# The second weight pair as seven half-size products, with GpSimd rebuilding two operand blocks

## The chip, the cores and the metric

The kernel runs on one core of a Trainium2 chip. Its time is device microseconds of one execution; the runs shown before are three, and their median is used. Five engines work side by side, each through a queue of its own in program order: TensorE (PE in the profile, its weight loads PEld), VectorE (DVE), ScalarE (ACT), GpSimd (POOL) and SyncE (SP), which here issues nearly all DMAs.

## The reference

One layer (DEPTH is 1, so only the short-convolution mixer runs), on 1024 tokens of 1024 channels, in float32:

```python
def short_conv_mixer(u, w_in, conv_w, w_out):
    z, bg, cg, v = jnp.split(u @ w_in.astype(u.dtype), 4, axis=-1)
    y = bg * causal_dwconv(cg * v, conv_w) * jax.nn.silu(z)
    return y @ w_out.astype(u.dtype)

h = x
u = rms_norm(h, pre_norm[i])
m = short_conv_mixer(u, sc_w_in[j], sc_conv_w[j], sc_w_out[j])
h = h + rms_norm(m, post_norm[i])
```

`w_in` is 1024 x 8192: four types (z, bg, cg, v) of 2048 columns. `conv_w` has 3 taps, `w_out` is 2048 x 1024.

## The kernel before

**Precision.** TensorE multiplies in a rounded 32-bit form (F32R). Each operand is held as two parts, a high part (a rounded copy, made by ScalarE) and a low part (what is left, a subtraction on VectorE); each product is three matmuls: high x high, high x low, low x high. One matmul is 128x128 weights against 128x512.

**Pairs and seven products.** The 2048 channels are 16 chunks of 128. For each chunk there are two weight pairs: p even holds types cg and v, p odd holds z and bg; so 32 pairs, `PAIRS`. Of a pair, the two types (rows n = 0, 1) times the two halves of the 1024 input channels make a 2x2 block of weights, and the two halves of the channels times the two halves of the tokens make a 2x2 block of the normalised input. The product of the two is done as in Strassen's and Winograd's scheme, with seven products `a, b, c, e, d, f, g` (ORDER) in place of eight: `product(p, i)` issues 4 x 3 matmuls. The weights enter as the plain row 0 (part 0, for a and b), as sums that GpSimd makes (`add_s`, L123 to L137; part 1 for c and e, part 2 for d and f) and as half of row 1 (part 3, for g); `split_w` (L143 to L155) splits each into its parts with one cast on ScalarE (L140) and one subtraction on VectorE (L141). The input side has seven operands too, in `UH[i]` and `UL[i]`: a and b are the two channel halves for the first 512 tokens, f and e come from the last 512, c, d and g are sums of these blocks. `snap`, `after` and `first_chunk` combine the products' banks and go on to the gate, the convolution and the next stage.

**The head.** The first two pairs, p = 0 and 1, are not done by seven products but plainly, in 2 types x 2 halves of the tokens x 8 slices x 3 = 96 matmuls each (`plain`, `high_plain`, `low_plain`), since the input's sums aren't there yet. The first four tiles of 128 tokens are loaded, normalised and transposed first (`turn`); a and b follow from them; the plain products of pair 0 on the first half of the tokens run on TensorE. Meanwhile the last four tiles get their squares (`square` on ScalarE at L323, `square_v` on VectorE at L326), the root and the reciprocal (`pre_rstd`, L86 to L105, with three tiny VectorE operations L103, L104, L105), and are scaled by these (L457 on VectorE, L459 on ScalarE). Then four rounds follow: `turn2(kk)` transposes two slices of the four tiles (8 small matmuls at L344), and `second(kk)` (L473 to L478) makes slices of the operands e and f from them. `rebuild(q)` (L405) adds the high and the low part of a or b into `bt`, which lies in the memory of the first input tiles `xa`; `second` subtracts `bt`'s first half from the fresh slice, `t_sub` makes c, d and g's sources of both halves. `t_split` splits these in two parts.

**Order.** The tile framework runs with `manual_schedule`: on every engine the instructions stand in program order, and only waits for data and for buffers are put in. Buffers come from pools with a fixed number of slots: tag "raw" has three (a pair's weights, 1 MB each), tag "sum" one (the weights' sums), tag "w8" three and "w4" two (split weights); a new tile waits until the slot's last reader is done. TensorE's program order in the head is: plain products of pair 0 on the first token half; four times (12 matmuls of pair 1, `turn2`, `second`); the rest of pair 1; pair 0 on the second token half; then pair 2 by seven products, and so on through pair 31, and the output product, which is done in the same seven-product form.

Of the kernel before, what the change touches and what calls it, by code (L numbers as in the profile page):

```python
# [8 lines left out]
F32 = mybir.dt.float32  # L9
F32R = mybir.dt.float32r  # L10
# [8 lines left out]
def kernel(  # L19
# [16 lines left out]
    nc = tc.nc  # L36
# [76 lines left out]
    def fetch(p, rows=(0, 1)):  # L113
        if p >= len(PAIRS):
            return
        c, tys = PAIRS[p]
        if p not in raws:
            raws[p] = raw.tile([P, 2, NK, P], F32, tag="raw", name=f"raw_{p}")
        for n in rows:
            c0 = tys[n] * CI + c * P  # L120
            nc.sync.dma_start(raws[p][:, n], wiv[:, :, c0 : c0 + P])
# [21 lines left out]
    def split_w(p, part):  # L143

        if p >= len(PAIRS):
            return
        n = 2 * HB if part < 3 else HB
        tag = "w8" if part < 3 else "w4"
        t = wp.tile([P, 2, n], F32R, tag=tag, name=f"w{part}_{p}", bufs=3 if part < 3 else 2)
# [172 lines left out]
    def square(t):  # L322
        nc.scalar.activation(junk, xs[t], AF.Square, scale=D ** -0.5, accum_out=sq[:, t : t + 1])  # L323
# [39 lines left out]

    plain_w = {}

    def tile_plain(p, n):
        if (p, n) == (1, 1):
            plain_w[p, n] = raw.tile([P, 2, D], F32R, tag="sum", name=f"wn{n}_{p}", bufs=1)
        else:
            plain_w[p, n] = wp.tile([P, 2, D], F32R, tag="w8", name=f"wn{n}_{p}", bufs=3)  # L370

    def high_plain(p, n):
        tile_plain(p, n)
        nc.scalar.copy(plain_w[p, n][:, 0], flat(raws[p][:, n]))

    def low_plain(p, n):
        t = plain_w[p, n]
        nc.vector.tensor_sub(t[:, 1], flat(raws[p][:, n]), t[:, 0].bitcast(F32))

    def plain(p, n, half, part, kks=range(4)):  # L380
# [4 lines left out]
        for kk in kks:  # L385
            k = part * KH + kk
            hi, lo = (w[:, h, k * P : (k + 1) * P] for h in (0, 1))
            nc.tensor.matmul(ps, hi, UH[i][:, kk], start=part == 0 and kk == 0, stop=False, skip_group_check=True)  # L388
            nc.tensor.matmul(ps, hi, UL[i][:, kk], start=False, stop=False, skip_group_check=True)  # L389
            nc.tensor.matmul(ps, lo, UH[i][:, kk], start=False, stop=kk == KH - 1, skip_group_check=True)  # L390
# [9 lines left out]
    def rebuild(q, js=(0, 1)):  # L400

        for j in js:
            ks = slice(2 * j, 2 * j + 2)
            i = "ab"[q]
            nc.vector.tensor_add(bt[:, q, ks], UH[i][:, ks].bitcast(F32), UL[i][:, ks].bitcast(F32))  # L405


    stir(WARM)
# [22 lines left out]
    high_plain(0, 1)  # L431
    low_plain(0, 1)
    for k in range(KH):
        plain(0, 0, 0, 0, [k])
        for t in (2, 3) if k < KH - 1 else range(TH):
            turn(k + KH, t)
    read_k(4)
# [16 lines left out]
    for j in range(TH):  # L454
        x2 = xs[TH + j]
        if j % 2:
            nc.vector.tensor_scalar(x2, x2, rs2[:, j : j + 1], None, op0=ALU.mult)  # L457
        else:
            nc.scalar.activation(x2, x2, AF.Copy, scale=rs2[:, j : j + 1])  # L459
    low_plain(1, 1)  # L460
    rebuild(0, [1])


    def turn2(kk):
        for k in (kk, kk + KH):
            for t in range(TH, NT):
                turn(k, t)
# [9 lines left out]
        low("f", kk, p22, kk + KH)  # L477
        nc.vector.tensor_sub(by_tile(UL["e"][:, kk]), t1, by_tile(UH["e"][:, kk]).bitcast(F32))  # L478
# [12 lines left out]
    def halves(a, j):  # L491
        return a[:, 2 * j : 2 * j + 2].rearrange("p k (t l) -> p k t l", t=TH)

    def t_split(i, src):
        for j in range(2):
            hi, lo = (halves(u[i], j) for u in (UH, UL))
            nc.scalar.copy(hi, src(j))
            nc.vector.tensor_sub(lo, src(j), hi.bitcast(F32))

    def t_sub(q):  # L500
        for j in range(2):
# [22 lines left out]
    pc = bank("pcw")  # L524
    nc.tensor.transpose(pc[:, : TAPS * NC], cw_rows, ident[: TAPS * NC, : TAPS * NC])
    nc.scalar.copy(cw, pc[:, : TAPS * NC])
# [25 lines left out]

    def first_chunk(i):

        if i == "b":
            g = gpad[:, TAPS - 1 : TAPS - 1 + HB]
            nc.scalar.copy(g, banks[0, 0, 0])
            nc.vector.tensor_mul(g, banks[0, 1, 0], g)
            nc.vector.tensor_mul(gpad[:, TAPS - 1 + HB :], sn[0, 0], sn[0, 1])
        elif i == "c":  # L560
            conv(0)
        elif i == "d":
            cv, z = cvs.pop(0), banks[1, 0, 0]
            nc.scalar.activation(z, z, AF.Silu)
            nc.scalar.activation(sn[1, 0], sn[1, 0], AF.Silu)
            nc.vector.tensor_mul(cv[:, :HB], banks[1, 1, 0], cv[:, :HB])
            nc.vector.tensor_mul(cv[:, :HB], z, cv[:, :HB])
            nc.gpsimd.tensor_mul(cv[:, HB:], cv[:, HB:], sn[1, 1])
            nc.gpsimd.tensor_mul(cv[:, HB:], cv[:, HB:], sn[1, 0])
            y_done(0, cv)  # L570


# [34 lines left out]
    END = len(PAIRS) - 1  # L607
    TODO = {p: p // 2 - 2 for p in range(4, 4 + 2 * CH - 2, 2)}
    TODO[2 * CH + 1] = CH - 1
    for p in range(2, len(PAIRS)):  # L610
        q, prev = p + 1, p // 2 - 1
        for i in ORDER:
# [180 lines left out]
```

## Time and profile before

| | |
|---|---|
| three runs | 795.88, 795.68, 795.34 us; median 795.68 |
| profiled execution | 796.12 us, span of its instructions 794.3 us |
| matmuls and other TensorE instructions | 3514, busy 99% of the span |
| VectorE, ScalarE, GpSimd busy | 67%, 39%, 34% |
| mean granted TensorE clock | 0.998 |
| DMA | 114.38 MB, 144 GB/s on average |

A row of the timeline is: start (us from the span's start), duration, engine, line, operation, what is written <- what is read, shape, count, and in brackets how long the engine stood idle before it and what ended that. Rows of one kind in a row are merged (x2 and more). A row's duration includes the time in which the instruction itself is held up inside the engine; a next one of the same engine can start a little before the end of the one before. Matmuls show 0.39 us each but follow each other more closely, as they are pipelined. In the table of stretches the columns are the stretch, its length, then for each engine the busy time and count, the granted clock, the DMA share and GB/s.

### The profile page before, as it was taken

Reading aid. Unit: us, or ns where it says so; the run is one execution under the profiler, and the core shown is the slowest. Engines: PE = TensorE matmul, PEld = TensorE weight load, DVE = VectorE, ACT = ScalarE, POOL = GpSimd, SP = SyncE. Lnnn points to the kernel's source line nnn. Section 1 sums busy time; section 2 is a strip of 40 time slices with the busy share of each in tenths; the row PEclk is TensorE's granted clock in tenths of the full one; section 3 lists DMA queues with packets and bytes.
Section 4 is the critical chain, followed back from the end, with each engine's and each line's share of the span. In section 5 each row is a group of like instructions: output and inputs, shape, how many; then the busy total and the mean of one; then the engine's idle time right before and its main releaser. Section 6 shows DMA issues by size and latency. Waiting matters only on the chain.

```text
span 794.3 us, 9053 instructions
## 1 busy us (share of the span) xinstructions
PE 785.7 (99%) x3514; PEld 652.1 (82%) x3514; DVE 534.8 (67%) x580; ACT 306.6 (39%) x421; POOL 271.2 (34%) x182
## 2 busy tenths in 40 slices
PE   9999999999999999999999999999999999999996
PEld 8888888888888888888888888888888888888885
DVE  5899676767676767676757666666666857633766
ACT  6636333342433333333333332323333536544441
POOL 0034534443444444447444444444344000000020
PEclk9999999999999999999999999999999999999999
DMA  9600361517070707165433334142515659555237
GB/s 317 161 0 1 93 198 54 199 53 229 23 242 10 252 26 226 45 207 174 130 94 106 109 91 145 54 142 57 161 39 178 233 193 419 204 203 212 106 111 260
DMA packets 94282, 114.38 MB, mean 144 GB/s; under 512 B 2920, under 2 KB 68512, under 8 KB 92192
## 3 DMA queue, kind: packets, MB, share of 16 engines
q1 hardware_dynamic: 94224, 113.81, 44.1%
q8 instruction: 27, 0.44, 0.2%
q14 instruction: 15, 0.12, 0.0%
q10 hardware_dynamic: 16, 0.00, 0.0%
HBM read 84.44 MB, written 29.36 MB: 143 GB/s over the span
## 4 chain that ended last, share of the span: by engine, by line
PE 94%; DMA 3%; DVE 1%; ACT 1%; SPq 0%; POOLq 0%; POOL 0%; issue 0%; DVEq 0%; ACTq 0%
PE px L186 14%; PE px L187 14%; PE px L188 14%; PE pv L186 7%; PE pv L187 7%; PE pv L188 7%; PE py L186 3%; PE py L187 3%; PE py L188 3%; PE po_x L673 3%; PE po_x L672 3%; PE po_x L671 3%; PE pp L389 2%; PE pp L390 2%; PE pp L388 2%; DMA xr<-in_x 2%
## 5 line engine op out<-in xcount | busy, mean ns | idle before, releaser
L141 DVE TENSOR_TENSOR w<-sum,w 128x1024 fp32r<-128x1024 f32 x60 | 89.8, 1498 | 75.1 <-ACT w L140 75.1
L141 DVE TENSOR_TENSOR w<-raw,w 128x1024 fp32r<-128x1024 f32 (+1 forms) x60 | 96.6, 1609 | 5.2 <-ACT w L140 5.2
L140 ACT CAST w<-sum 128x1024 fp32r<-128x1024 f32 x60 | 62.9, 1048 | 56.6 <-issue 54.5
L548 DVE SCALAR_TENSOR_TENSOR cv<-gpad,cw,cv 128x1024 f32<-128x1024 f32 x32 | 63.2, 1976 | 19.7 <-ACT cv L546 19.1
L140 ACT CAST w<-raw 128x1024 fp32r<-128x1024 f32 (+1 forms) x60 | 49.9, 832 | 62.6 <-PE py L188 62.6
L133 POOL TENSOR_TENSOR sum<-raw 128x512 f32<-128x512 f32 x30 | 39.1, 1302 | 90.5 <-PE pp L390 51.5
L225 POOL TENSOR_TENSOR gpad<-snc,sne 128x512 f32<-128x512 f32 x15 | 19.4, 1295 | 139.6 <-DVE snc L220 139.6
L136 POOL TENSOR_TENSOR sum<-raw 128x512 f32<-128x512 f32 x30 | 59.8, 1992 | 0.0
L220 DVE TENSOR_TENSOR snc<-pv,snc 128x512 f32<-128x512 f32 x30 | 20.7, 691 | 54.1 <-PE pv L188 54.1
L217 POOL TENSOR_TENSOR sne<-sne,cv 128x512 f32<-128x512 f32 x15 | 19.4, 1293 | 103.1 <-DVE sne L215 103.1
L137 POOL TENSOR_TENSOR sum<-raw,sum 128x512 f32<-128x512 f32 x30 | 53.9, 1796 | 0.0
L711 POOL TENSOR_TENSOR acc<-acc,xr 128x512 f32<-128x512 f32 x4 | 6.9, 1722 | 133.0 <-DVE acc L710 133.0
L186 PE MATMUL px<-u_g,w 128*128 128x512 f32 x120 | 46.8, 390 | 0.0
L188 PE MATMUL px<-u_g,w 128*128 128x512 f32 x120 | 46.7, 390 | 0.0
L188 PE MATMUL pv<-u_f,w 128*128 128x512 f32 x120 | 46.7, 390 | 0.0
L186 PE MATMUL pv<-u_f,w 128*128 128x512 f32 x120 | 46.7, 389 | 0.0
L187 PE MATMUL pv<-u_f,w 128*128 128x512 f32 x120 | 46.7, 389 | 0.0
L187 PE MATMUL px<-u_g,w 128*128 128x512 f32 x120 | 46.7, 389 | 0.0
L187 PE MATMUL py<-u_b,w 128*128 128x512 f32 x120 | 46.7, 389 | 0.0
L186 PE MATMUL py<-u_b,w 128*128 128x512 f32 x120 | 46.7, 389 | 0.0
L187 PE MATMUL px<-u_a,w 128*128 128x512 f32 x120 | 46.7, 389 | 0.0
L186 PE MATMUL px<-u_a,w 128*128 128x512 f32 x120 | 46.7, 389 | 0.0
(248 smaller groups left out, 2092.5 us busy)
## 6 DMA issues: line engine op xcount, KB each, us to landing
raw<-in_sc_w_in SPq DMA_DIRECT2D x64, 512.0 KB, 5.9
y_d<-cv SPq DMA_DIRECT2D x16, 512.0 KB, 3.3
t<-in_sc_w_out SPq DMA_DIRECT2D x8, 1024.0 KB, 5.8
t_d<-t SPq DMA_DIRECT2D x8, 1024.0 KB, 4.5
s_d<-s SPq DMA_DIRECT2D x8, 768.0 KB, 3.5
s<-y_d SPq DMA_DIRECT2D x8, 512.0 KB, 5.0
xr<-in_x SPq DMA_DIRECT2D x8, 512.0 KB, 4.6
out<-acc SPq DMA_DIRECT2D x12, 256.0 KB, 2.4
```

The costliest lines, as they stand in the source:

```text
L133: nc.gpsimd.tensor_add(s[:, 1], a21, a22)
L136: nc.gpsimd.tensor_sub(s[:, 2], a11, a21)
L137: nc.gpsimd.tensor_sub(s[:, 3], a12, s[:, 0])
L140: nc.scalar.copy(hi, src)
L141: nc.vector.tensor_sub(lo, src, hi.bitcast(F32))
L186: nc.tensor.matmul(ps, lo, UH[i][:, k], start=first and k == 0, stop=False, skip_group_check=True)
L187: nc.tensor.matmul(ps, hi, UL[i][:, k], start=False, stop=False, skip_group_check=True)
L188: nc.tensor.matmul(ps, hi, UH[i][:, k], start=False, stop=last, skip_group_check=True)
L548: nc.vector.scalar_tensor_tensor(cv, gpad[:, j : j + L], tap(c, j), cv, op0=ALU.mult, op1=ALU.add)
L671: nc.tensor.matmul(ps, lo, u[:, 0, k], start=first, stop=False, skip_group_check=True)
L672: nc.tensor.matmul(ps, hi, u[:, 1, k], start=False, stop=False, skip_group_check=True)
L673: nc.tensor.matmul(ps, hi, u[:, 0, k], start=False, stop=last, skip_group_check=True)
```

## The change

Pair 0 stays plain. Pair 1 is done by seven products, in an order interleaved with the second half of pair 0: product a, `turn2(0)`, product b, `turn2(1)`, then pair 0's products on the second token half in four pieces (`plain_late(kk)`, one slice of f and of e each, with `turn2(2)` and `turn2(3)` between them), then c, e, d, f, g. The weights of pair 1 therefore go through `add_s` and `split_w`, where `high_plain` and `low_plain` stood; parts 1 and 2 of them are put into slots of tag "raw". `rebuild` is on GpSimd in place of VectorE, all four steps of it, three of them earlier in the order (`rebuild(0, [1])` now stands ahead of the scaling, and `rebuild(1)`, which stood behind the operand d, just behind the scaling). The sums of pair 2 (`add_s(2, ...)`) move up between the rounds. The load of pair 2's weights stands later in program order, and the small transpose that prepares the convolution's taps stands ahead of product a. `t_halves` is the two steps of `t_split`, so that the sum of product e's and d's banks can be put between them for g. `first_chunk` follows the new names, and the remaining splits of pair 2 move into it.

```diff
+        if p == 1 and part in (1, 2):
+            t = raw.tile([P, 2, n], F32R, tag="raw", name=f"w{part}_{p}")
+        else:
+            t = wp.tile([P, 2, n], F32R, tag=tag, name=f"w{part}_{p}", bufs=3 if part < 3 else 2)
...
     fetch(1)
     nc.sync.dma_start(cw_rows, conv_w[0].rearrange("t (c p) -> (t c) p", p=P))
-    fetch(2)
...
     def rebuild(q, js=(0, 1)):
...
-            nc.vector.tensor_add(bt[:, q, ks], UH[i][:, ks].bitcast(F32), UL[i][:, ks].bitcast(F32))
+            nc.gpsimd.tensor_add(bt[:, q, ks], UH[i][:, ks].bitcast(F32), UL[i][:, ks].bitcast(F32))
...
     plain(0, 0, 0, 1)
     plain(0, 1, 0, 1)
-    high_plain(1, 0)
     rebuild(0, [0])
+    add_s(1, 0)
     square(TH)
     square_v(TH + 1)
-    low_plain(1, 0)
+    split_w(1, 0)
     square(TH + 2)
     square_v(TH + 3)
     rs2 = pre_rstd(list(range(TH, NT)))
-    high_plain(1, 1)
+    add_s(1, 1)
+    rebuild(0, [1])
     for j in range(TH):
...
-    low_plain(1, 1)
-    rebuild(0, [1])
+    rebuild(1)
+    split_w(1, 1)
+    pc = bank("pcw")
+    nc.tensor.transpose(pc[:, : TAPS * NC], cw_rows, ident[: TAPS * NC, : TAPS * NC])
+    nc.scalar.copy(cw, pc[:, : TAPS * NC])
...
-    for kk, (n, part) in enumerate(((0, 0), (1, 0), (0, 1), (1, 1))):
-        plain(1, n, 0, part)
-        turn2(kk)
-        second(kk)
-        if part == 0:
-            plain_snap(1, n)
+    def plain_late(kk):
+
+        for part in (1, 0):
+            for n in (0, 1):
+                plain(0, n, 1, part, [kk], first=part == 1 and kk == 0, last=part == 0 and kk == KH - 1)
+
+    product(1, "a")
+    snap(1, "a")
+    turn2(0)
+    second(0)
+    split_w(1, 3)
+    fetch(2)
+    product(1, "b")
+    after(1, "b")
+    turn2(1)
+    second(1)
+    split_w(1, 2)
+    plain_late(0)
+    turn2(2)
+    second(2)
+    add_s(2, 0)
+    add_s(2, 1)
+    plain_late(1)
+    turn2(3)
+    second(3)
+    plain_late(2)
+    plain_late(3)
...
-    for kks in ((0, 1, 2), (3,)):
-        for n in (0, 1):
-            plain(1, n, 1, 0, kks)
-    for n in (0, 1):
-        plain(1, n, 1, 1)
     t_split("c", lambda j: cols4(1, j))
     t_sub(0)
     t_split("d", lambda j: halves(bt[:, 0], j))
-    plain_add(1, 0)
-    rebuild(1)
-    plain_add(1, 1)
+    product(1, "c")
+    snap(1, "c")
     t_sub(1)
     new_u("g")
-    add_s(2, 0)
+    product(1, "e")
+    snap(1, "e")
+    product(1, "d")
+    g_hi, g_lo = t_halves("g", lambda j: halves(bt[:, 1], j))
+    g_hi(0)
+    g_lo(0)
+    g_hi(1)
+    nc.vector.tensor_add(sn[1, "e"], banks[1, "x"], sn[1, "e"])
+    g_lo(1)
+    product(1, "f")
+    product(1, "g")
     split_w(2, 0)
-    t_split("g", lambda j: halves(bt[:, 1], j))
...
+    plain_add(0, 0)
+    plain_add(0, 1)
+    nc.vector.tensor_add(sn[1, "c"], banks[1, "v"], sn[1, "c"])
     head.close()
...
     fetch(3)
-
-    for n in (0, 1):
-        for part in (0, 1):
-            plain(0, n, 1, part)
-    add_s(2, 1)
-    split_w(2, 3)
-    split_w(2, 1)
-    split_w(2, 2)
-    plain_add(0, 0)
-    plain_add(0, 1)
```

More of the change, by code (lines that the diff above doesn't have):

```diff
@@ L364 @@
     plain_w = {}
[L366 to L370, printed above, removed]
     def high_plain(p, n):
-        tile_plain(p, n)
+        plain_w[p, n] = wp.tile([P, 2, D], F32R, tag="w8", name=f"wn{n}_{p}", bufs=3)
         nc.scalar.copy(plain_w[p, n][:, 0], flat(raws[p][:, n]))
@@ L378, in low_plain, with plain @@
         nc.vector.tensor_sub(t[:, 1], flat(raws[p][:, n]), t[:, 0].bitcast(F32))
-    def plain(p, n, half, part, kks=range(4)):
+    def plain(p, n, half, part, kks=range(4), first=None, last=None):
         i = "abef"[2 * half + part]
@@ L384, in plain @@
         ps, w = banks[p, n, half], plain_w[p, n]
-        for kk in kks:
+        first = part == 0 if first is None else first
+        last = part == 1 if last is None else last
+        for j, kk in enumerate(kks):
             k = part * KH + kk
             hi, lo = (w[:, h, k * P : (k + 1) * P] for h in (0, 1))
-            nc.tensor.matmul(ps, hi, UH[i][:, kk], start=part == 0 and kk == 0, stop=False, skip_group_check=True)
+            end = last and j == len(kks) - 1
+            nc.tensor.matmul(ps, hi, UH[i][:, kk], start=first and j == 0, stop=False, skip_group_check=True)
             nc.tensor.matmul(ps, hi, UL[i][:, kk], start=False, stop=False, skip_group_check=True)
-            nc.tensor.matmul(ps, lo, UH[i][:, kk], start=False, stop=kk == KH - 1, skip_group_check=True)
+            nc.tensor.matmul(ps, lo, UH[i][:, kk], start=False, stop=end, skip_group_check=True)
     def plain_snap(p, n):
@@ L433 @@
     for k in range(KH):
-        plain(0, 0, 0, 0, [k])
+        plain(0, 0, 0, 0, [k], first=k == 0)
         for t in (2, 3) if k < KH - 1 else range(TH):
@@ L492, in halves, with t_halves @@
         return a[:, 2 * j : 2 * j + 2].rearrange("p k (t l) -> p k t l", t=TH)
+    def t_halves(i, src):
+        hi, lo = ((lambda j, u=u: halves(u[i], j)) for u in (UH, UL))
+        return (
+            lambda j: nc.scalar.copy(hi(j), src(j)),
+            lambda j: nc.vector.tensor_sub(lo(j), src(j), hi(j).bitcast(F32)),
+        )
     def t_split(i, src):
+        hi, lo = t_halves(i, src)
         for j in range(2):
-            hi, lo = (halves(u[i], j) for u in (UH, UL))
-            nc.scalar.copy(hi, src(j))
-            nc.vector.tensor_sub(lo, src(j), hi.bitcast(F32))
+            hi(j)
+            lo(j)
     def t_sub(q):
@@ L553, in first_chunk @@
     def first_chunk(i):
-        if i == "b":
+        if i == "":
             g = gpad[:, TAPS - 1 : TAPS - 1 + HB]
@@ L609 @@
     TODO[2 * CH + 1] = CH - 1
+    first_chunk("")
     for p in range(2, len(PAIRS)):
```

27 lines of the change are left out of this document (14 added, 13 removed).

## The prediction

> **What bounds the kernel now.** I read the page first, then the table of stretches, the waits of TensorE (PE), and the timelines of the first 64 us engine by engine.
>
> ```profile
> PE 785.7 (99%) x3514; PEld 652.1 (82%) x3514; DVE 534.8 (67%) x580; ACT 306.6 (39%) x421; POOL 271.2 (34%) x182
> ```
>
> ```profile
> PE pp L389 <- DVE u_a L357: 0.5, 1, 0.5
> ```
>
> ```profile
> 63.89 0.39 PE L186 MATMUL px<-u_a,w 128*128 128x512 f32 x1
> ...
> 66.61 0.39 PE L186 MATMUL py<-u_b,w 128*128 128x512 f32 x1
> ```
>
> TensorE is busy for 99% of the span. The second line is the only wait of TensorE in 13:700 us. So the kernel is a dense line of matmuls: one removed saves its slot, and a hole in the line costs its full length. The slot is the distance of the third fence: twelve matmuls from 63.89 to 66.61, so 0.227 us each (the 0.39 us of one overlaps its neighbours).
>
> **What is removed.** The pair takes 2 types x 2 halves of the tokens x 8 slices x 3 = 96 matmuls now and 7 products x 4 slices x 3 = 84 afterwards. 12 x 0.227 = **-2.72 us**. The transposes and the rest of TensorE's list keep their number. That is all the change can gain while TensorE stays fed.
>
> **What is moved to GpSimd (POOL).** The four rebuild steps of 128x1024 leave VectorE (DVE), and four sums of 128x512 for this pair are new, as the weights now enter as sums. GpSimd waits for nothing there but its data, so it runs as soon as it can. In what order VectorE and GpSimd get on beside each other is decided by these rows:
>
> ```profile
> 67.61 1.30 POOL L133 TENSOR_TENSOR sum<-raw 128x512 f32<-128x512 f32 x1 [6.51 <-DVE w L141]
> ```
>
> ```profile
> 52.84 1.56 POOL L133 TENSOR_TENSOR sum<-raw 128x512 f32<-128x512 f32 x1 [51.51 <-PE pp L390]
> 54.48 2.15 POOL L134 TENSOR_TENSOR sum<-sum,raw 128x512 f32<-128x512 f32 x1
> 56.60 2.27 POOL L136 TENSOR_TENSOR sum<-raw 128x512 f32<-128x512 f32 x1
> ```
>
> ```profile
> 53.16 2.32 DVE L405 TENSOR_TENSOR xa<-u_b 128x1024 f32<-128x1024 f32 x1
> 55.41 0.68 DVE L398 TENSOR_TENSOR sp<-pp,sp 128x512 f32<-128x512 f32 x1
> ```
>
> A sum alone takes 1.30 us. A VectorE operation of 128x1024 with both inputs in SBUF alone takes 1.2 (21.59, below), and its successor starts 1.14 later. Side by side they take turns, whole instructions at a time: the VectorE one of 53.16 needs 2.32 = what is left of GpSimd's (to 54.4) + 1.1; GpSimd's of 54.48 needs 2.15 = what is left of VectorE's (to 55.4) + 1.25. The one of 55.41 reads one input from PSUM and keeps its 0.68 beside a busy GpSimd. Even a tiny operation queues, as the end of the kernel shows:
>
> ```profile
> 772.70 1.73 POOL L711 TENSOR_TENSOR acc<-acc,xr 128x512 f32<-128x512 f32 x1 [2.02 <-DVE acc L710]
> ```
>
> ```profile
> 773.51 0.15 DVE L99 TENSOR_SCALAR hr_post<-r_post 128x1 f32<-128x1 f32 x1
> 773.58 0.87 DVE L101 SCALAR_TENSOR_TENSOR nt_post<-r_post,ve_post 128x1 f32<-128x1 f32 x1
> 774.48 0.16 DVE L105 SCALAR_TENSOR_TENSOR rs_post<-nt_post,hr_post 128x1 f32<-128x1 f32 x1
> ```
>
> L101, one element per partition, ends at 774.45, just as GpSimd's operation does at 774.43; L105, of the same kind but behind it, takes 0.16. L99, with one tensor input, doesn't wait (0.15). So where GpSimd has a queue, every VectorE operation with two SBUF inputs, however small, waits for one GpSimd operation: 1.27 us for 512 elements, and about 2.5 for a rebuild of 1024. The 2.5 is an estimate, twice the 512 row; bounds are 1.8 (a fixed share of it paid once) and 3.0.
>
> **Who waits behind that.** The second half of the tokens is normalised at just this place. Before:
>
> ```profile
> 21.59 1.21 DVE L405 TENSOR_TENSOR xa<-u_a 128x1024 f32<-128x1024 f32 x1
> 22.72 1.22 DVE L326 SCALAR_TENSOR_TENSOR u_e<-xb 128x1024 fp32r<-128x1024 f32 x1
> ...
> 23.86 1.22 DVE L378 TENSOR_TENSOR wn<-raw,wn 128x1024 fp32r<-128x1024 f32 x1
> 25.00 1.22 DVE L326 SCALAR_TENSOR_TENSOR u_e<-xb 128x1024 fp32r<-128x1024 f32 x1
> ...
> 26.94 0.15 DVE L103 TENSOR_TENSOR nt_pre<-r_pre 128x4 f32<-128x4 f32 x1
> 27.13 0.16 DVE L104 TENSOR_TENSOR nt_pre<-nt_pre,ve_pre 128x4 f32<-128x4 f32 x1
> 27.33 0.17 DVE L105 SCALAR_TENSOR_TENSOR rs_pre<-nt_pre,hr_pre 128x4 f32<-128x4 f32 x1
> 27.53 1.42 DVE L457 TENSOR_SCALAR xb<-xb,rs_pre 128x1024 f32<-128x1024 f32 x2
> ```
>
> ```profile
> 23.45 1.06 ACT L323 ACTIVATE junk<-xb 128x1024 f32<-128x1024 f32 x1
> 24.41 0.19 ACT L323 ACTIVATION_READ_ACCUMULATOR junk<-xb 128x1 f32 x1
> ...
> 27.53 2.19 ACT L459 ACTIVATE xb<-xb,rs_pre 128x1024 f32<-128x1024 f32 x2
> ```
>
> ```profile
> 29.99 1.03 PE L344 MATMUL pk<-ident,xb 128*128 128x128 f32 x8
> ```
>
> The chain is: squares, root, reciprocal, three tiny VectorE operations (L103 to L105, each with two SBUF inputs), then the scaling, half on ScalarE (ACT, to 29.72), then the transposes at 29.99. TensorE's cover is one block of 12 matmuls, which ends at 29.99 and in the new order (product a, behind one small transpose) at about 30.1. It hides 0.3 us of delay and no more.
>
> GpSimd's new list starts once the transposes that read the tile it overwrites are done:
>
> ```profile
> 18.20 1.05 PE L342 MATMUL pk<-rows,xa 128*128 128x128 f32 x8
> ```
>
> ```profile
> 10.64 3.84 SPq L121 DMA_DIRECT2D raw<-in_sc_w_in  x2
> ```
>
> ```profile
> DMA to landing us min/median/max: 5.7/9.2/10.7
> ```
>
> So from 19.3. The pair's weights, issued from 10.64 with at most 10.7 us to landing, are there at about 21.8 (issue of the second at 11.1). With turns taken as above, estimated from the rows:
>
> - GpSimd: first rebuild 19.3-21.8. VectorE: first square 21.8-23.0. GpSimd: sum 1 23.0-24.2, sum 2 24.3-25.6, as VectorE has nothing ready: its weight rounding waits for ScalarE's cast, which is now behind a square (ends about 24.6).
> - VectorE: weight rounding 25.6-26.7. GpSimd: sum 3 to 28.0. VectorE: second square to 29.1. GpSimd: sum 4 to 30.4.
> - The root and the reciprocal need no turn (29.1-29.8). L103 at 30.4. Rebuild 2 to 33.0. L104. Rebuild 3 to 35.7. L105, ready at 35.9. Rebuild 4 to 38.4.
> - ScalarE scales two tiles, 35.9 to 38.1 (2.19 before). The transposes start at **38.1** instead of 30.1, a hole of **+8.0 us** in TensorE's line.
>
> **Is the hole closed later?** No: TensorE has no slack from there to 760. Nor does it grow, by VectorE's load from the scaling to the first use of c:
>
> ```profile
> 31.13 0.74 DVE L473 SCALAR_TENSOR_TENSOR xb<-pk,gcol,xa 128x512 f32<-128x512 f32 x1
> ...
> 33.31 0.68 DVE L478 TENSOR_TENSOR u_e<-xb,u_e 128x512 fp32r<-128x512 f32 x1
> ```
>
> Four rounds of 2.9 (31.13 to 33.99), three roundings at 1.14 (the sums' two parts, c's first half), and two operations of 512 elements at 0.6: about 16.2 us, against four groups of transposes of 0.9 (the 1.03 of 29.99 overlaps its successor) and 60 matmuls of 0.227 = 17.2 on TensorE. That is covered by 1.1 us, and more while TensorE runs at half clock (next). The sums for the third pair wait for the one sum buffer and so come after this pair's rounding. The loads of the fourth and fifth weight pair now wait for buffers that this pair's products e and f read, but are wanted one pair and more later. Both cost nothing as long as TensorE is the late one; without that cover, each GpSimd operation in VectorE's way costs 1.27.
>
> **The clock.** These rows say what a hole does to TensorE's clock:
>
> ```profile
> 1.05 5.48 PE L320 MATMUL pw<-idle 128*128 128x128 f32 x28 [1.05 <-DVE idle L280]
> 6.87 1.83 PE L342 MATMUL pk<-rows,xa 128*128 128x128 f32 x14 [0.34 <-DVE rows L412]
> ```
>
> ```profile
> 785.00:794.30 9.30, 2.65 (x12) 1.87 (x10) 4.74 (x15) 0.98 (x3) 0.00 (x0) 0.80 0.61 212
> ```
>
> In the last 9.3 us TensorE works 2.65 and the mean clock is 0.80. If idle means half, that is 3.7 us at half, so the clock falls about 3 us after the last matmul. A hole of 8 us is longer. At the start 28 matmuls take 5.48 us and 14 later ones 1.83 (0.11 apart): with 0.21 for a slow one, 20 were slow, so the slow stretch lasts 4.4 us. At half speed that loses **+2.2 us**. The Trainium skill ("TensorE: Matmul & The Clock Gate", What's actually happening) has the clock restored after one busy window of about 3.4 us; by that this term would be an estimated 1.7 and the forecast 0.5 lower. The trace's 4.4 is used.
>
> **Sum**: -2.72 + 8.0 + 2.2 = **+7.5 us**. The profiled execution is 796.12 (span 794.3), 0.44 above the median of the runs, 795.68; so I expect 803.6 for a profiled one and **803.2** as the time.
>
> **Rivals.**
>
> 1. *VectorE's scaling (L457) waits as well.* It has one tensor input, as L99, which didn't wait; but its two of 1024 take 1.42, twice the pace of the others, so it may use both paths. Then the scaling behind rebuild 4 ends at 39.8 instead of 38.1: 804.9. The Trainium skill ("SBUF — State Buffer", Who interferes with whom) says this of tensor_scalar in its two-port modes, and that the later one fully blocks; no run here shows L457 beside GpSimd. Chance 0.20.
> 2. *The tiny operations slip between GpSimd's.* For it: they hold the path for 0.15 only. Against: 773.58. Then the root's result comes at 30.4, the transposes start at 32.6, hole 2.5, no cold clock: 795.5. But the three rebuilds left then fall on the VectorE rounds, where up to one wait of 2.5 stays uncovered: 798.0. Chance 0.13.
> 3. *Faster.* The squares find gaps and the root's result is there by 27.9, when ScalarE's 2.19 still ends under product a. That is the point from which it decides. For it: VectorE is rid of the 1.14 of rebuild that stood ahead of the first square (21.59). Against: GpSimd has over 10 us of queue by then. Gain 2.72: 793.0. Chance 0.13.
> 4. *VectorE stays behind.* Slow rebuilds (3.0) and the sums for pair three hit c, d and g too: two or three waits of 1.27 more, 806 to 807. Chance 0.04.
>
> **Numbers.** Forecast 0.50. About 0.2% (1.6 us) is what a measurement can tell from no change, so "same" is 794.1 to 797.3: a third of rival 2, 0.05 with its edges. Faster is rival 3, 0.13; slower 0.82. The range runs from 796.5 (between the ends of rival 2) to 806.5: rebuilds of 1.8 us give -1.0, of 3.0 +1.4, a clock that never drops -2.2, rival 1 +1.7. What it leaves out is rival 3 and bits of rivals 2 and 4.
>
> **What would show it.** In the new profile TensorE should have one wait of 8 us ahead of L344, its clock under 1.0 in the slice behind it, L103 to L105 at up to 2.5 us each with GpSimd busy between 19 and 38, and matmul groups 12 fewer. The prediction is wrong if the transposes start by 31, if the root's operations keep their 0.15 beside GpSimd, or if holes appear at c or g instead.

## The result and the profile after

| | before | after |
|---|---|---|
| median of five runs | 795.68 us (795.34 to 796.19) | 804.46 us (804.07 to 806.75) |
| profiled execution, span | 796.12, 794.3 | 804.46, 802.7 |
| mean granted clock | 0.998 | 0.994 |

The changed kernel is slower, 1.0116 times the time before (95% interval 1.0101 to 1.0131), 8.8 us by the medians and 8.3 us by the two profiled executions. Each ratio further down is against the kernel before on the same chip, where its median was 795.77, 796.07 or 796.10 us. In the changed file the lines have moved by some places: the transposes of the second half of the tokens are L346 (L344 before), the products' matmuls L189 to L191 (L186 to L188), the scaling L458 and L460 (L457 and L459).

The page of after, busy time and the granted clock in 40 slices:

```profile
PE 785.1 (98%) x3502; PEld 649.8 (81%) x3502; DVE 538.4 (67%) x579; ACT 308.6 (38%) x424; POOL 286.2 (36%) x190
...
PEclk9899999999999999999999999999999999999999
```

TensorE has the 12 matmuls less (3514 to 3502) and is busy for the same time, but in a longer span. Its waits in 13:700 us (us in total, times, longest):

```profile
PE pk L346 <- ACT xb L460: 8.2, 2, 7.9
PE pv L189 <- ACT sne L197: 0.5, 1, 0.5
```

Before, there was one wait of 0.5, at the first operands; it is still there and not shown. New is one hole of 7.9 us ahead of the transposes, named after ScalarE's scaling. ScalarE itself waited (all engines' waits, after):

```profile
ACT xb L460 <- DVE rs_pre L105: 7.7, 1, 7.7
ACT sne L197 <- POOL cv L593: 3.8, 1, 3.8
```

So the reader goes on to VectorE, the timeline of after:

```profile
29.01 1.06 DVE L97 TENSOR_SCALAR ve_pre<-sq 128x4 f32<-128x4 f32 x1
...
30.18 2.19 DVE L99 TENSOR_SCALAR hr_pre<-r_pre 128x4 f32<-128x4 f32 x1
32.28 0.15 DVE L103 TENSOR_TENSOR nt_pre<-r_pre 128x4 f32<-128x4 f32 x1
32.47 2.19 DVE L104 TENSOR_TENSOR nt_pre<-nt_pre,ve_pre 128x4 f32<-128x4 f32 x1
34.69 2.26 DVE L105 SCALAR_TENSOR_TENSOR rs_pre<-nt_pre,hr_pre 128x4 f32<-128x4 f32 x1
36.98 1.42 DVE L458 TENSOR_SCALAR xb<-xb,rs_pre 128x1024 f32<-128x1024 f32 x2
```

and of GpSimd beside it:

```profile
27.77 2.27 POOL L137 TENSOR_TENSOR sum<-raw,sum 128x512 f32<-128x512 f32 x1
30.00 2.34 POOL L405 TENSOR_TENSOR xa<-u_a 128x1024 f32<-128x1024 f32 x1
32.30 4.63 POOL L405 TENSOR_TENSOR xa<-u_b 128x1024 f32<-128x1024 f32 x2
```

The ends stand next to each other. VectorE's L97 ends at 30.07, as GpSimd's last sum does at 30.04; L99, on four elements per partition, ends at 32.37 and the rebuild of 30.00 at 32.34. L104 ends at 34.66 and L105 at 36.95; GpSimd's last two rebuilds fill 32.30 to 36.93. L99, L104 and L105 each take the time of one rebuild, about 2.2 us in place of 0.16. The scaling then runs with GpSimd out of the way, in its usual 1.42.

TensorE's timeline of after from the transposes on, and the start of the fourth pair before:

```profile
38.19 0.69 PE L346 MATMUL pk<-ident,xb 128*128 128x128 f32 x2 [7.87 <-ACT xb L460]
39.23 1.54 PE L346 MATMUL pk<-ident,xb 128*128 128x128 f32 x6 [0.35 <-ACT xb L460]
...
44.00 1.03 PE L346 MATMUL pk<-ident,xb 128*128 128x128 f32 x8
...
47.62 1.03 PE L346 MATMUL pk<-ident,xb 128*128 128x128 f32 x8
...
51.23 1.03 PE L346 MATMUL pk<-ident,xb 128*128 128x128 f32 x8
...
57.81 0.39 PE L189 MATMUL px<-u_c,w 128*128 128x512 f32 x1
...
71.42 0.39 PE L189 MATMUL px<-u_a,w 128*128 128x512 f32 x1
...
91.44 0.39 PE L189 MATMUL px<-u_a,w 128*128 128x512 f32 x1
```

```profile
82.93 0.39 PE L186 MATMUL px<-u_a,w 128*128 128x512 f32 x1
```

From these rows the 8.34 us between the spans can be laid out. Pair 2's product a starts 7.53 later than before (71.42 against 63.89). That is the hole of 7.87, less 2.72 for the 12 matmuls, plus 2.42: from the first transposes to product c there are 19.62 us (38.19 to 57.81), where TensorE's own list is 17.2 (the prediction's count of transposes and matmuls; a run below shows 17.23). These three make 7.57. Pair 2 then takes 20.02 where it took 19.04 (63.89 to 82.93): +0.98. From there to the end 0.17 is regained.

The 2.42 lies almost wholly in the first of the four rounds: 38.19 to 44.00 is 5.81, and the two behind it are 3.62 and 3.61, which is the eight transposes and twelve matmuls at their usual pace. The clock at this place (stretch, length, PE, PEld, DVE, ACT, POOL busy, clock, DMA), after:

```profile
35.00:40.00 5.00, 1.46 (x6) 1.06 (x7) 3.37 (x3) 3.02 (x3) 1.93 (x1) 0.52 0.00 0
40.00:45.00 5.00, 5.00 (x25) 4.28 (x24) 4.34 (x6) 2.52 (x6) 0.00 (x0) 0.80 0.01 2
```

0.80 over 40 to 45 is 2.0 us at half, so the clock is low until about 42.0, 3.8 us into the work. So far all of it reads like the prediction. Whether the low clock is what costs the 2.42 is asked below.

### The profile page after: what moved, and what is told of

It reads as the page before. It is cut to its first block, busy times and chain, and to the rows that moved or that the text cites. A ratio compares the mean times of both kernels' runs of the same rounds, so it can differ in the third digit from the quotient of the medians.

```text
span 802.7 us, 9045 instructions
## 1 busy us (share of the span) xinstructions
PE 785.1 (98%) x3502; PEld 649.8 (81%) x3502; DVE 538.4 (67%) x579; ACT 308.6 (38%) x424; POOL 286.2 (36%) x190
## 4 chain that ended last, share of the span: by engine, by line
PE 92%; DVE 2%; issue 2%; DMA 2%; ACT 1%; POOL 1%; SPq 0%; DVEq 0%; POOLq 0%
PE px L189 13%; PE px L190 13%; PE px L191 13%; PE pv L189 7%; PE pv L190 7%; PE pv L191 7%; PE po_x L704 4%; PE po_x L703 4%; PE po_x L702 4%; PE py L189 3%; PE py L190 3%; PE py L191 3%; PE po_v L704 2%; PE po_v L703 2%; PE po_v L702 2%
## 5 line engine op out<-in xcount | busy, mean ns | idle before, releaser
L141 DVE TENSOR_TENSOR w<-sum,w 128x1024 fp32r<-128x1024 f32 x62 | 91.7, 1478 | 82.1 <-ACT w L140 82.0
L141 DVE TENSOR_TENSOR w<-raw,w 128x1024 fp32r<-128x1024 f32 (+1 forms) x62 | 99.1, 1600 | 7.0 <-ACT w L140 7.0
L140 ACT CAST w<-sum 128x1024 fp32r<-128x1024 f32 x62 | 65.0, 1048 | 58.3 <-issue 54.5
L133 POOL TENSOR_TENSOR sum<-raw 128x512 f32<-128x512 f32 x31 | 40.1, 1294 | 71.9 <-DVE w L141 69.8
L136 POOL TENSOR_TENSOR sum<-raw 128x512 f32<-128x512 f32 x31 | 62.6, 2020 | 0.0
L189 PE MATMUL pv<-u_f,w 128*128 128x512 f32 x124 | 48.4, 390 | 0.5 <-ACT sne L197 0.5
L189 PE MATMUL py<-u_b,w 128*128 128x512 f32 x124 | 48.7, 393 | 0.0
L191 PE MATMUL py<-u_b,w 128*128 128x512 f32 x124 | 48.5, 391 | 0.0
L190 PE MATMUL py<-u_b,w 128*128 128x512 f32 x124 | 48.5, 391 | 0.0
L189 PE MATMUL px<-u_a,w 128*128 128x512 f32 x124 | 48.4, 390 | 0.0
L189 PE MATMUL px<-u_g,w 128*128 128x512 f32 x124 | 48.3, 390 | 0.0
L190 PE MATMUL px<-u_g,w 128*128 128x512 f32 x124 | 48.3, 389 | 0.0
L191 PE MATMUL px<-u_g,w 128*128 128x512 f32 x124 | 48.3, 389 | 0.0
L190 PE MATMUL pv<-u_f,w 128*128 128x512 f32 x124 | 48.2, 389 | 0.0
L191 PE MATMUL px<-u_a,w 128*128 128x512 f32 x124 | 48.2, 389 | 0.0
```

The source lines that it names most:

```text
L133: nc.gpsimd.tensor_add(s[:, 1], a21, a22)
L136: nc.gpsimd.tensor_sub(s[:, 2], a11, a21)
L140: nc.scalar.copy(hi, src)
L141: nc.vector.tensor_sub(lo, src, hi.bitcast(F32))
L189: nc.tensor.matmul(ps, lo, UH[i][:, k], start=first and k == 0, stop=False, skip_group_check=True)
L190: nc.tensor.matmul(ps, hi, UL[i][:, k], start=False, stop=False, skip_group_check=True)
```

## The experiments

**The rebuilds alone on GpSimd.** The kernel before, with one word changed; nothing of the second weight pair is touched, and GpSimd makes no sums at this place.

```diff
-            nc.vector.tensor_add(bt[:, q, ks], UH[i][:, ks].bitcast(F32), UL[i][:, ks].bitcast(F32))
+            nc.gpsimd.tensor_add(bt[:, q, ks], UH[i][:, ks].bitcast(F32), UL[i][:, ks].bitcast(F32))
```

> The kernel before, plain products kept, with only the four rebuild steps moved to GpSimd at their old places in the program. GpSimd has no data to wait for, so it runs all four back to back from 18.6 us on. Theory: squares, one weight rounding and the root wait behind them by turns, the root is done near 32 us instead of 27.5, the transposes start near 34.5 instead of 30, a hole of 4 to 5 us in TensorE and a stretch at half clock behind it: 799 to 803 us. Rival (moving work off a two thirds busy VectorE to an idle GpSimd is free, the loss comes with the seven-product form): 795 to 796 us.

Measured: 802.81 us, 1.0088 (1.0074 to 1.0102), so +7.0 for this alone, within what was expected. The timeline of VectorE, of GpSimd, and TensorE's wait in this run:

```profile
24.72 3.41 DVE L378 TENSOR_TENSOR wn<-raw,wn 128x1024 fp32r<-128x1024 f32 x1
28.05 3.42 DVE L326 SCALAR_TENSOR_TENSOR u_e<-xb 128x1024 fp32r<-128x1024 f32 x1
```

```profile
23.67 6.72 POOL L405 TENSOR_TENSOR xa<-u_b 128x1024 f32<-128x1024 f32 x2
```

```profile
PE pk L344 <- ACT xb L459: 3.6, 2, 3.2
```

An operation that took 1.22 takes 3.41 when it stands behind a rebuild: 1.14 + 2.3. Here the rebuilds fall on the squares and one rounding, not on the tiny operations. The rule is the same: VectorE's two-input operation and GpSimd's take turns, whole instructions at a time. Which operations are hit depends on what is next on each side when a rebuild starts.

The 7.0 us are more than the hole. TensorE's first round in this run, and the end of the first round in the kernel before:

```profile
33.99 0.69 PE L344 MATMUL pk<-ident,xb 128*128 128x128 f32 x2 [3.21 <-ACT xb L459]
...
40.86 1.04 PE L344 MATMUL pk<-ident,xb 128*128 128x128 f32 x8
```

```profile
33.60 1.03 PE L344 MATMUL pk<-ident,xb 128*128 128x128 f32 x8
```

The transposes start 4.0 later (33.99 against 29.99), and the round behind them takes 6.87 in place of 3.61. The granted clock is 0.50 from 35 to 40 us, and VectorE waits 2.16 us for the next transposes. So here TensorE at the low clock is the late one, and the low clock costs about 3.3. The two parts make nearly all of the 7.4 us between the spans (801.7 and 794.3).

**The rebuilds back on VectorE.** The changed kernel with only that word undone; the sums and the new order stay.

```diff
-            nc.gpsimd.tensor_add(bt[:, q, ks], UH[i][:, ks].bitcast(F32), UL[i][:, ks].bitcast(F32))
+            nc.vector.tensor_add(bt[:, q, ks], UH[i][:, ks].bitcast(F32), UL[i][:, ks].bitcast(F32))
```

> The changed kernel with the four rebuild steps back on VectorE, at the places that the change gives them; GpSimd keeps only the pair's four sums there. Theory (turns between VectorE and GpSimd, whole instructions): two rebuilds of 1.14 us now stand in VectorE's own list ahead of the scaling, and three sums of 1.27 are still in turns with the squares and the root; the transposes start near 33 to 34 us instead of 38.2 in the changed kernel, the hole is some 3.5 to 4.5 us. Time 798 to 801 us, better than with GpSimd by 4 to 6 us, still slower than before by 2 to 5. Rival (it is VectorE's load that counts, so rebuilds on it must be worse than on GpSimd): 805 us or more.

Measured: 800.07 us, 1.0051 (1.0038 to 1.0065), within what was expected: +4.0 against the kernel before on its chip, so 4.8 of the 8.8 us go. The tiny operations and TensorE's waits:

```profile
28.09 1.06 DVE L97 TENSOR_SCALAR ve_pre<-sq 128x4 f32<-128x4 f32 x1
...
29.26 1.13 DVE L99 TENSOR_SCALAR hr_pre<-r_pre 128x4 f32<-128x4 f32 x1
```

```profile
PE pk L346 <- ACT xb L460: 1.9, 1, 1.9
PE pp L389 <- DVE u_f L359: 1.2, 2, 1.0
```

L97 and L99 now each wait for a sum of 512 (L99 1.13 in place of 2.19), L104 and L105 meet no GpSimd operation and take 0.16, and the hole is 1.9. Between the transposes at 32.08 and product c at 52.74 there are 20.66 us, 3.5 over TensorE's own list; VectorE has the two rebuilds of b's block to do there on top of its rounds. About half of the loss is the rebuilds' place on GpSimd, then; the other half is the rest of the change, with the rebuilds' earlier places in it.

**GpSimd kept out while the root is computed.** A tiny GpSimd operation that reads the root's result stands ahead of the second sums and of three rebuilds, so all of that queue starts behind L105.

```diff
     rs2 = pre_rstd(list(range(TH, NT)))
+    gate = small.tile([P, TH], F32, tag="gate", name="gate", bufs=1)
+    nc.gpsimd.tensor_add(gate, rs2, rs2)
     add_s(1, 1)
```

> The changed kernel with one tiny GpSimd addition that reads the root's result, put ahead of the pair's third sum: GpSimd does its first rebuild and two sums as before and then waits until the root is done. Theory (the small VectorE operations of the root each wait for one GpSimd operation): only the first two sums are left in their way, the root is done about 9 us earlier (near 28 to 29 us), the second half's first transposes start near 30 to 31 instead of 38.2, TensorE's hole there falls from 7.9 to about 1 us and its clock stays up. GpSimd's queue then falls on the four rounds that follow, which costs some 1 to 2 us of new holes there. Time 796 to 799 us. Rival (the hole comes of the new order on TensorE or of late weights, not of GpSimd's queue): no change, 803 to 806 us.

Measured: 800.25 us, 1.0058 (1.0042 to 1.0073); 1.3 above the upper end of what was expected. VectorE, GpSimd, and TensorE's waits:

```profile
27.96 0.16 DVE L105 SCALAR_TENSOR_TENSOR rs_pre<-nt_pre,hr_pre 128x4 f32<-128x4 f32 x1
28.16 2.50 DVE L460 TENSOR_SCALAR xb<-xb,rs_pre 128x1024 f32<-128x1024 f32 x2
...
35.39 2.63 DVE L484 TENSOR_TENSOR u_e<-xb,u_e 128x512 fp32r<-128x512 f32 x1
37.95 2.85 DVE L141 TENSOR_TENSOR w<-raw,w 128x512 fp32r<-128x512 f32 x1
```

```profile
35.10 5.16 POOL L405 TENSOR_TENSOR xa<-u_b 128x1024 f32<-128x1024 f32 x2
```

```profile
PE pk L346 <- DVE sna L213: 2.0, 1, 2.0
PE pp L389 <- DVE u_e L484: 0.9, 1, 0.9
```

The tiny operations have their 0.16 again, the transposes start at 30.27, and the hole is gone: the cause of the 7.87 is shown. But 4.5 us stay. The rebuilds now stand beside the rounds, and two operations of 512 elements take 2.63 and 2.85 instead of 0.68. The stretch from the transposes to product c (53.71) grows to 23.44, 6.2 over TensorE's own list: 3.5 are TensorE's waits, and behind those of 0.9 and 2.0 the granted clock is low again (0.53 from 42.50 to 46.10). Put behind the root, the rebuilds hold up the rounds instead. The scaling also shows that the prediction's first rival is a real mechanism: with one tensor input it takes 2.50 for two beside GpSimd, against 1.42 alone. It just did not meet GpSimd in the changed kernel.

**The clock kept up through the hole.** Dummy matmuls on idle data behind product a keep TensorE busy until the transposes. The diff has 64 calls; a second run has 32.

```diff
     snap(1, "a")
+    pw2 = bank("pw2")
+    for _ in range(64):
+        nc.tensor.matmul(pw2[:, :P], idle, idle, start=True, stop=True, skip_group_check=True)
     turn2(0)
```

> The changed kernel with 64 small matmuls on zeros between product a and the first transposes of the second half, some 7 us, all inside the hole of TensorE and read by nothing. Theory: the hole's length for useful work stays, the transposes start at 38.2 as before, but the clock isn't lowered, so the half-clock stretch (35.2 to 42.0 us in the changed kernel, with matmuls from 38.2 on) goes: 1.5 to 2.2 us less, 802.2 to 803.0 us. If the clock costs nothing because VectorE sets the pace of these rounds anyway: no change, 804 to 805 us.

Measured: 808.67 us, 1.016 (1.0146 to 1.0174), and not what was meant: one call is two instructions, so the dummies ran 14.46 us, 6.6 beyond the hole. The run answers another question, though. TensorE's timeline in it:

```profile
30.51 14.46 PE L494 MATMUL pw<-idle 128*128 128x128 f32 x128
44.80 1.04 PE L346 MATMUL pk<-ident,xb 128*128 128x128 f32 x8
...
62.03 0.39 PE L189 MATMUL px<-u_c,w 128*128 128x512 f32 x1
```

Transposes to product c: 17.23, TensorE's own list and nothing else. With the clock up, and with 6.6 us more for VectorE to get ahead, the 2.42 are gone, and a start that is 6.61 later than in the changed kernel makes the span only 4.3 longer (807.0 against 802.7).

> The changed kernel with 32 calls of a small matmul on zeros behind product a. Each call is two instructions in the profile, 0.11 us apart, so 7.1 us in all, from about 30.1 to 37.2, inside the hole of the changed kernel (30.1 to 38.2) and read by nothing. Theory: the transposes start at 38.2 as before and the clock isn't lowered, so what the half clock took goes: 1.5 to 2.2 us less, 802.2 to 803.0 us. If VectorE sets the pace of these rounds anyway: no change, 804 to 805 us.

Measured: 804.62 us, 1.0108 (1.0094 to 1.0121), +8.6 against the kernel before on its chip, where the changed kernel had +8.8. The theory of a clock term asked for 802.2 to 803.0, the rival that VectorE sets the pace for 804 to 805. The clock, the rounds and TensorE's waits:

```profile
40.00:45.00 5.00, 4.94 (x28) 3.96 (x26) 4.21 (x6) 3.24 (x7) 0.00 (x0) 1.00 0.01 2
```

```profile
38.32 0.44 PE L346 MATMUL pk<-ident,xb 128*128 128x128 f32 x2 [0.78 <-ACT xb L460]
...
42.81 1.04 PE L346 MATMUL pk<-ident,xb 128*128 128x128 f32 x8
...
46.78 1.03 PE L346 MATMUL pk<-ident,xb 128*128 128x128 f32 x8
...
50.75 1.03 PE L346 MATMUL pk<-ident,xb 128*128 128x128 f32 x8
...
57.98 0.39 PE L189 MATMUL px<-u_c,w 128*128 128x512 f32 x1
```

The differences of these starts, beside those of after and of the 64 calls:

| from the transposes of one round to the next, us | 1 | 2 | 3 | 4, to product c | sum |
|---|---|---|---|---|---|
| after, clock low until 42.0 | 5.81 | 3.62 | 3.61 | 6.58 | 19.62 |
| 32 calls, clock up | 4.49 | 3.97 | 3.97 | 7.23 | 19.66 |
| 64 calls, clock up, VectorE ahead | 3.65 | 3.61 | 3.62 | 6.35 | 17.23 |

(The last row's starts between 44.80 and 62.03 are 48.45, 52.06 and 55.68.) With the clock up, the first round gains 1.3, and the three later ones lose it again (0.35, 0.36 and 0.65), as TensorE catches up with VectorE and waits for the low part of f. So the low clock cost nothing that VectorE's list would not have cost anyway: two causes lie over each other, and taking this one away changes nothing. That is so in this kernel; with the rebuilds alone on GpSimd, where VectorE had time to spare, the low clock cost 3.3.

**The rounds without three rebuilds.** The gate kernel above with `rebuild(0, [1])` and `rebuild(1)` left out, so three of the four rebuilt blocks are missing from the computation.

```diff
     add_s(1, 1)
-    rebuild(0, [1])
...
-    rebuild(1)
     split_w(1, 1)
```

> As e1_gate (GpSimd waits for the root ahead of the third sum), with three of the four rebuild steps left out, so that the operands e, f, c, d and g are made from other data; part of the computation is missing. In e1_gate the first rebuild behind the gate and its two followers stood in the way of two VectorE operations of 512 elements, which took 2.6 and 2.85 us, and TensorE had 3.5 us of holes at the second and third round. Theory: these holes go with the rebuilds, what is left is half a microsecond in pair 3, and the 2.72 us of matmuls saved show at last: 793.5 to 796 us. Rival (the holes come of the two sums or of the new order): 798 to 800 us.

Measured: 795.94 us, 0.9999 (0.999 to 1.0009): the time before, at the upper edge of the range, although 12 matmuls are gone and there is no hole; the 2.72 us that were to show at last do not. The stretch from its transposes to its product c:

```profile
30.00:49.06 19.06, 18.55 (x93) 14.54 (x92) 17.55 (x23) 10.01 (x16) 7.06 (x5) 1.00 0.00 1
```

It takes 19.06 us with the clock at 1.00, 1.9 over TensorE's own list, and VectorE is busy for 17.55 of them. So VectorE sets the pace of the rounds even with no rebuild in its way, and 1.9 of the 2.72 us are lost there. Pair 2 takes 20.03 in this run too (62.70 to 82.73), and that takes the rest.

**The 12 matmuls by themselves.** The kernel before, with 12 matmuls of pair 0 left out of the computation.

```diff
-            plain(0, n, 1, part)
+            plain(0, n, 1, part, range(4) if part else (0, 3))
```

> The kernel before with 12 matmuls of 128x512 left out of the first pair's products for the second half of the tokens (two of the eight slices of both types), so part of the computation is missing. It measures what 12 matmuls in a TensorE line without holes are worth. Theory: 12 x 0.227 = 2.7 us less, 792.8 to 793.3 us. Rival (the operands of the seventh product or the next pair's weights are late then, so part of it turns into a wait): 793.5 to 795.5 us.

Measured: 794.64 us, 0.9985 (0.9976 to 0.9994): 1.1 us, where 2.72 of TensorE's time were taken out. The new wait:

```profile
PE px L186 <- DVE w L141: 0.9, 1, 0.9
```

Pair 2's first weights now come late from VectorE: their rounding ends at 62.42, and the product starts at 62.48. In the kernel before it ended at 62.18, 1.7 ahead of its use. VectorE is the second bound here, and most of the removal runs into it. The place counts: this run takes the matmuls out of pair 0, just ahead of pair 2, the change takes them out of pair 1.

**A version with the parts put right.** From these: both rebuild steps of a's block at once, ahead of the squares; b's block not rebuilt but copied from PSUM by ScalarE; GpSimd's sums behind the last scaled tile; one rounding later; one more buffer for the banks' copies.

```diff
-        t = snp.tile([P, HB], F32, tag="sn", name=f"sn{i}_{p}", bufs=5)
+        t = snp.tile([P, HB], F32, tag="sn", name=f"sn{i}_{p}", bufs=6)
...
+    def keep(k):
+        nc.scalar.activation(bt[:, 1, k - KH], pk[k, 0], AF.Copy, scale=gcol[:, k : k + 1])
...
-    rebuild(0, [0])
-    add_s(1, 0)
+    rebuild(0)
...
+    keep(4)
+    keep(5)
     rs2 = pre_rstd(list(range(TH, NT)))
-    add_s(1, 1)
-    rebuild(0, [1])
+    keep(6)
...
-    rebuild(1)
-    split_w(1, 1)
+    keep(7)
+    gate = small.tile([P, TH], F32, tag="gate", name="gate", bufs=1)
+    last = xs[NT - 1][:, :TH]
+    nc.gpsimd.tensor_add(gate, last, last)
+    add_s(1, 0)
+    add_s(1, 1)
...
     split_w(1, 2)
+    split_w(1, 1)
```

> The changed kernel with GpSimd kept out of VectorE's way: the rebuild of a (two steps) right away, while VectorE works from PSUM or waits for weights; the copy of b for the later subtraction made by ScalarE straight from the transposed tiles in PSUM, in its idle time around the root, so no third and fourth rebuild; GpSimd waits until the last tile is scaled before it makes the pair's sums; these sums' first part is rounded a round later; one more buffer for the products' copies. Theory: the transposes start near 30 to 30.5 us with no hole over 0.5 us, sums cost VectorE two or three waits of up to 1.25 us in the rounds, the seven products' 2.72 us are kept in part: 794 to 796 us. If VectorE's list as such is too long for the new order (its load from the scaling to product g leaves hardly 1 us): 796 to 798 us. If GpSimd's queue wasn't the cause: over 800 us.

Measured: 796.61 us, 1.0008 (0.9999 to 1.0016). The transposes start at 29.83 and there is no hole, but product c comes at 49.46, 19.63 later, and a wait in pair 2 has moved rather than gone:

```profile
PE px L189 <- DVE sne L218: 0.6, 1, 0.6
```

The time lies in the range of the rival, by which VectorE's list is too long for this order. How much of that is the list itself, and how much GpSimd's sums in its way (a rounding of 512 elements took 1.77 in place of 0.68 beside one), this run does not separate.

**The convolution and one rounding moved.** The same, with the first chunk's convolution step one product earlier, and the first rounding behind the squares:

```diff
     square_v(TH + 1)
-    split_w(1, 0)
     square(TH + 2)
     square_v(TH + 3)
+    split_w(1, 0)
...
-        elif i == "a":
             conv(0)
+        elif i == "a":
             split_w(2, 2)
```

> As e8_best, with two moves: the first convolution (one ScalarE and two VectorE operations) is issued ahead of the copy of pair 2's first product instead of behind it, and the second square stands ahead of the rounding of the first weights on both engines. In e8_best VectorE stood idle for 1.6 us there for ScalarE and 13 us later TensorE waited 0.8 us for VectorE at pair 2's product g. Theory: that wait goes, pair 2 takes 19.1 us again as in the kernel before, and 0.5 to 1.3 us of e8_best's time with it: 795.2 to 796.1 us, so at or just under the kernel before. Rival (the wait at g comes of GpSimd's sums beside VectorE's rounding, not of the late convolution): same as e8_best, 796.3 to 796.9 us.

Measured: 795.46 us against 796.10 before on the same chip, 0.9993 (0.9984 to 1.0001); within what was expected. Of its twelve runs one took 3103 us, which the ratio leaves out, the others 794.93 to 796.17. Its pair 2 (the stretch from one product a to the next):

```profile
62.74:81.78 19.04, 19.04 (x86) 15.77 (x84) 16.60 (x18) 9.55 (x12) 11.51 (x7) 1.00 0.38 109
```

Pair 2 is back at 19.04. In the version above, with the sixth buffer but the old order, it took 19.94 (63.06 to 83.00). So the +0.98 is not something that seven products must cost: the two moves take it away, and of the two the convolution's stands inside pair 2. This version is 9.0 us under the changed kernel by the medians. That it beats the kernel before is not shown, as the interval holds 1.

## Why the prediction was right, and where its steps were off

The time came out near the forecast (804.46 against 803.2), by the mechanism that was named. A part of the closeness is luck: in the hole two errors of about 1 us cancel, and the clock's term stands for time that VectorE's list would have taken as well.

- **The bound.** Up to the hole TensorE's line was the bound, and 7.87 - 2.72 + 2.42 accounts for pair 2's start to 0.04 us. Behind the hole VectorE is as late as TensorE, which the prediction did not see: the gate run, without the hole, gives back 4.3 us and not 8.
- **The hole, +8.0.** Measured 7.87, by the mechanism named: the gate run takes it away, and moving the rebuilds alone brings one. The way there differed. A rebuild takes 2.33, not 2.5. L97 and L99, which the prediction let pass because L99 at the end of the kernel had not waited, took 1.06 and 2.19. L103 slipped in behind L99 in 0.15. The chain so met the fourth rebuild too, which the prediction let run behind it, and L105 ended at 36.95 rather than 35.9. What made this good is that the first transposes need only the first of ScalarE's two tiles: they started 1.24 behind L105, not 2.2, and the second tile cost the 0.35 that is part of the 2.42. The two errors have nothing to do with each other; that they cancel is luck.
- **The rule for one tensor input failed.** It was read from a row of 128x1. Rows of 128x4 and of 128x1024 wait. The Trainium skill ("SBUF — State Buffer", Who interferes with whom) has it that tensor_scalar can enter the modes that use the shared ports and that the later engine then blocks fully; the rows of 2.19 for 128x4 and of 2.50 for two of 128x1024 agree. Why the 128x1 of L99 did not wait, no run here isolates.
- **The clock, +2.2.** The place and the size look right: the first round is 2.2 longer than the next ones. As a term of its own it is wrong in this kernel. With the clock kept up the time is the same (804.62), since VectorE's list then takes the 2.4. As a mechanism it is real: with the rebuilds alone on GpSimd it costs 3.3. Nor is its size fixed. By the granted clock the low stretch lasts 6.8 us in both runs (35.18 to 42.01 and 33.25 to 40.08, worked out from stretches that it ends in), but TensorE's work begins 3.0 us into it in the one and 0.7 in the other.
- **The cover of 1.1 us. This is the step that failed.** The prediction set VectorE's 16.2 for the whole stretch against TensorE's 17.2. From the end of the scaling (36.98 + 1.42 = 38.40) VectorE, by its timeline in after, stood idle 1.74 for ScalarE's cast of the sums and 0.51 in the first round, and met one of pair 2's sums (1.19 for an operation of 0.68); none of this was in the 16.2:

```profile
40.14 1.23 DVE L141 TENSOR_TENSOR w<-sum,w 128x1024 fp32r<-128x1024 f32 x1 [1.74 <-ACT w L140]
...
42.54 0.75 DVE L479 SCALAR_TENSOR_TENSOR xb<-pk,gcol,xb 128x512 f32<-128x512 f32 x1 [0.51 <-DVE xb L477]
...
51.75 1.19 DVE L482 TENSOR_TENSOR u_e<-xb,u_e 128x512 fp32r<-128x512 f32 x1
```

  And the stretch was taken as one: the low part of f is wanted by the second matmul of every round's block, so the cover has to hold round by round. In the changed kernel TensorE did not wait in the later rounds because the low clock had put it as far back as VectorE. Had the clock not dropped, the prediction's way of adding would have given 2.2 less, and the 32 calls show that the time would have been the same.
- **Pair 2's sums and late loads "cost nothing".** TensorE did not wait for a load or a sum there, but pair 2 took 0.98 longer, with 0.5 of it at `pv` behind ScalarE's copy, which waited for a buffer that GpSimd's convolution step (L593) still read. The sum had no term for it.
- **The 2.72.** In the layout of the spans it stands in full, but the 2.42 next to it is time that VectorE takes back. Left out at another place, twelve matmuls were worth 1.1. Without the hole and without three of the rebuilds almost nothing of the 2.72 is left, and the version at the end has 0.6 of it, with an interval that holds 1.
- **The rivals.** The first did not come about in the changed kernel, since the last rebuild ended at 36.93 and the scaling began at 36.98, but the gate run shows its mechanism. The second is refuted by L99, L104 and L105; L103 alone slipped between. The third, a gain at 793.0, wanted the root's result by 27.9; it came at 36.95. Of the fourth, the rebuilds took 2.33 and not 3.0, and TensorE has no wait at c, d or g.
- **The sum.** +7.5 against +8.34 in the profiled executions: pair 2 is +0.98, the regained part -0.17. The rest to the 8.8 of the medians is the 0.44 by which the profiled execution of before lay above its median, while that of after lies on it.

Open: what lets L103 slip in while its neighbours wait, and whether the last version is faster than the kernel before. The two halves of the loss do not add up either: the rebuilds alone cost 7.0, the rest alone 4.0 (800.07 against 796.07), both together 8.8. A late TensorE leaves VectorE time in the rounds, as the 64 calls show, but no run measures how much of the 2.2 that is.

## What to carry to other kernels

In these traces work moved from VectorE to GpSimd did not run beside VectorE where both read two operands from SBUF. They took turns by whole instructions, so the price is about the number of VectorE instructions on the critical chain times GpSimd's instruction length, and a chain of tiny operations is the worst place for it. Keep long GpSimd operations away from such a chain by giving them something late to wait for, and look first whether there is a place with room at all. When TensorE is 99% busy, find the second bound before pricing a removal: leave the work out in one run and see how much of it comes back. A term of the sum can be shown by the rows and still be worth nothing, when a second engine is as late: keep that one cause away in a run before believing its size.

## What the hardware showed that was not expected

- Four elements per partition wait as long as a thousand: 2.19 and 2.26 us for 128x4 behind rebuilds of 2.33, against 0.16 alone, and with one tensor input too (L97 1.06, L99 2.19).
- The clock was low for 6.8 us behind a hole of 7.9 and for 6.8 us behind one of 3.2. The first, with 3.8 us of TensorE's work in it, cost nothing in the end, as VectorE's list was just as late; the second, with 6.1 us of work in it, cost 3.3.
- The clock fell 4.9 us after the last matmul in the changed kernel, 2.5 us after it with the rebuilds alone on GpSimd, and in the gate run behind waits of only 0.9 and 2.0 us.
- One call of a matmul on plain (not rounded) 32-bit data is two instructions, 0.113 us apart (14.46 us for 128).
